# Two projection tiles per group by seven half-size products, sums of u kept on chip, and gates and a partial output parked in DRAM, in a one-core hybrid layer

## The chip, the core and the metric

One Trainium2 chip, one core. The metric is the device time of one execution in microseconds (us); less is better. TensorE (PE) multiplies matrices into PSUM, VectorE (DVE) and ScalarE (ACT) work on elements, GpSimd (POOL) and SyncE (SP) here mostly issue DMAs. Each engine runs its own queue in order; a wait at the head of a queue holds what is behind it.

## The reference

One layer over 528 tokens (16 learned ones and 512 of input), model width 1024, everything float32. Cut to what matters here:

```python
h = concat([meta, x])                       # 528 x 1024
u = rmsnorm(h, mix_norm_w)
proj = u @ w_in                             # columns: pool 1024 | z 2048 | xbc 4096 | dt 32 | gates 2048
xbc = silu(causal_depthwise_conv(xbc, conv_w, conv_b))   # xs 2048, B 1024, C 1024
dt = softplus(dt_raw + dt_bias)
y = ssd_chunked(xs, dt, -exp(a_log), B, C) + xs * d_skip # 8 groups of 4 heads, 4 chunks of 128 tokens
y = group_rmsnorm(y * silu(z)) * ssd_norm_w
y_ssd = y @ w_ssd_out
y_pool = pool_mixer(u_pool) @ w_pool_up
h = h + (sigmoid(gate_p) * y_pool + sigmoid(gate_s) * y_ssd) @ w_o
h = h + relu(rmsnorm(h) @ w_ff1)**2 @ w_ff2
out = rmsnorm(h)[16:]
```

## The kernel before

Every float32 matrix product is made of three products of rounded parts: each operand is split into a high part (a cast to fp32r on ACT, for weights at L70) and a low part (the rest, a subtraction on DVE, for weights at L71), and PE adds high·high, high·low and low·high in PSUM. u lies in SBUF already split (`uh`, `ul`, the pair `U`), 128 model columns by 528 tokens in each of 8 tiles.

**Weights** come as blocks of 128x1024 in the order in which they are used, one DMA each on SP's queue (L69). A block has a `raw` tile (3 buffers) and after the split a `whi` and a `wlo` tile (4 buffers each). One block is one 128-column tile of `w_in`, all eight 128-row steps of the contraction.

**Groups.** The scan goes by 8 groups. `group_proj(g)` (L350) makes a group's inputs: tiles B (`bt`), C (`ct`), two x tiles (`xc`, 256 columns of x in all), for some groups a gate tile (`gate_pool`, L510), and two z tiles. B, C and x each are one `proj`: 8 steps of the contraction, in each two runs of 264 (C: 258) tokens, three matmuls a run, so 48 matmuls, into one two-bank PSUM tile of `psum2`, of which there are two. Then `conv` (L327) reads that PSUM tile: an ACT activation (L329) and three DVE operations (L332), and an ACT Silu (L334) on the result. The PSUM tile is free when the third DVE operation is done.

**Order.** `weave` (L499) alternates the steps of `ssd(g)`, the scan of group g, with those of `group_proj(g + 1)`; the final order on each engine is set when the program is built, from a model of the engines' times, and is fixed on the chip. In this text weave g is the stretch in which ssd(g) runs and the inputs of group g + 1 are made. Weaves 1, 2, 3 and 5 hold a gate, weave 4 also `out_half` (L538): the output projection of groups 0 to 3, eight tiles that ACT copies from PSUM to `acc`. Weave 7 has no group left to prepare and makes `out_part` (L547), which adds groups 4 to 6 to `acc` on DVE. `ssd` gets its decay row `abc` by a DMA on POOL's queue (L389), which waits until the previous group is done with the one buffer.

**Kept in SBUF for long:** `m1` (8 gate tiles of 128x512) and `acc` (8 tiles of 128x512). The pool branch later multiplies `m1[d]` by its own product (L647).

**Start.** x^T comes in 8 tiles on SP's queue; dt's weights (128x256) on ACT's queue behind the vector of constants (L180). PE runs nine matmuls on ones and then dt and the first B tile, step by step as x^T comes.

**Behind all this** are the pool branch, the output projections, `w_o`, and the MLP, whose second product already goes by Strassen's algorithm. None of them is edited, except where `m1` and `acc` come from.

Of the kernel before, what the change touches and what calls it, by code (L numbers as in the profile page):

```python
# [42 lines left out]
WARM = 9  # L43


@with_exitstack
def kernel(ctx: ExitStack, tc, xT, x, w, vec, fnw, out):
# [25 lines left out]
    def block():  # L73
        t = block_tiles()
        block_part(t, slice(0, 1024))
        return t[2:]

# [50 lines left out]
    m1p = y_stack.enter_context(tc.tile_pool(name="m1p", bufs=1, side="right", reuse_waits="tile"))  # L128
    m1 = [m1p.tile([P, SEQ], F32, name=f"m1_{d}") for d in range(NK)]
# [50 lines left out]
    nc.scalar.dma_start(raw[:, :256], w[b, :, :256])  # L180
# [138 lines left out]
    def norm_u():  # L319
        for k in range(NK):  # L320
            dve.scalar_tensor_tensor(xt[k], xt[k], col(V_MIX, k), rsb, op0=ALU.mult, op1=ALU.mult)
            act.copy(uh[k], xt[k])
            dve.tensor_tensor(ul[k], xt[k], uh[k].bitcast(F32), op=ALU.subtract)
# [25 lines left out]
    def group_proj(g, cur, gate=None):  # L349

        first = g == 0
        xc, bt, ct, zt = cur
        for dst, t, skip in ((bt, 16 + g, 0), (ct, 24 + g, NM - 4), (xc[:, 0, :], 2 * g, 0),
                             (xc[:, 1, :], 2 * g + 1, 0)):
# [26 lines left out]
    def ssd(g, cur):  # L381
# [99 lines left out]
        qh, ql = col_sums(f"g{g}", sq[:, 0, :], gs, ("qh", "ql"))  # L481
# [28 lines left out]
    def gate_pool(d, first=False):  # L510
        ps = psum2(f"pgp{d}")[:, :SEQ]
        proj(narrow(ps), block(), X if first else U)
        if first:
            dve.tensor_tensor(m1[d], ps, rsb[:, NM:], op=ALU.mult)
        act.activation(m1[d], m1[d] if first else ps, AF.Sigmoid, bias=col(V_BG, d))
# [13 lines left out]
    accp = y_stack.enter_context(tc.tile_pool(name="accp", bufs=1, side="right", reuse_waits="tile"))  # L529
    acc = [accp.tile([P, SEQ], F32, name=f"acc{d}") for d in range(NK)]  # L530
    ys = []

# [6 lines left out]
    def out_half():  # L539
        for dd in range(4):  # L540
            ps = psum2(f"pso{dd}")
            for i in range(2):
                ssd_out(2 * dd + i, ps[:, i * SEQ : (i + 1) * SEQ], range(8))
                act.copy(acc[2 * dd + i], ps[:, i * SEQ : (i + 1) * SEQ])
                yield

    def out_part():  # L547

        un = units()
        for d in range(NK):  # L550
# [3 lines left out]
            dve.tensor_tensor(acc[d], acc[d], ps, op=ALU.add)  # L554
            yield

    for g in range(G):
        nxt = group_tiles(g + 1) if g + 1 < G else None
        fill = [group_proj(g + 1, nxt, GATE_AT.get(g))] if nxt else [out_part()]
# [81 lines left out]
    for d in range(NK):  # L641
# [5 lines left out]
        dve.tensor_tensor(m1[d], m1[d], ps, op=ALU.mult)  # L647
# [410 lines left out]
```

## Time and profile before

| what | value |
|---|---|
| median of 3 runs | 1030.96 us (1030.59 to 1031.04) |
| profiled execution, whole time | 1030.68 us |
| its span in the trace | 1029.0 us (1.7 us lie outside) |
| granted TensorE clock | 1.00 throughout |
| busy: PE, DVE, ACT, POOL | 1019.9, 711.7, 541.2, 9.9 us |
| scan stretch, weaves 0 to 6 | 67.5 to 442.0 us |

A row of a view of the trace has the start, the duration, the engine (PEld is the weight load, which runs beside PE), the line, the operation, the tiles written and read with their shapes, a count, and in brackets the idle time of the engine before it with what ended it. In the view by windows a row gives the length of a stretch and the busy time and count of each engine in it.

### The profile page before, as it was taken

What the parts mean: (1) busy time and instruction counts of PE and PEld (TensorE: products, weight loads), DVE (VectorE), ACT (ScalarE), POOL (GpSimd) and SP (SyncE); (2) the same over time, 40 slices, a digit from 0 to 9 for tenths busy, and PEclk for the clock granted to TensorE, in tenths of its full rate; (3) what the DMA queues carried; (4) which work ended last, traced back from release to release, by engine and by line L of the source; (5) the groups of instructions that cost most, each with busy time, mean ns of one, the idle gap of its engine ahead of it and who ended that gap; (6) DMA issues with size and microseconds to landing.
All of it is one profiled execution on the core that took longest, in us unless ns stands there. A gap on an engine that the chain in (4) does not pass through costs nothing.

```text
span 1029.0 us, 14033 instructions
## 1 busy us (share of the span) xinstructions
PE 1019.9 (99%) x5721; PEld 881.8 (86%) x5721; DVE 711.7 (69%) x934; ACT 541.2 (53%) x706; POOL 9.9 (1%) x24
## 2 busy tenths in 40 slices
PE   9999999999999999999999999999999999999997
PEld 8889988998879898988998888888888888888886
DVE  7978788687637586878674345646686686776866
ACT  7765967586627349573443223344545355354444
POOL 0100000000000000000000000000000000000000
PEclk9999999999999999999999999999999999999999
DMA  7332051414332321413332323543223324334112
GB/s 234 100 132 104 20 165 41 145 56 129 102 117 69 107 99 41 148 54 117 94 92 94 103 84 101 204 136 130 86 83 120 114 75 122 100 102 124 42 41 82
DMA packets 29280, 105.62 MB, mean 103 GB/s; under 512 B 3296, under 2 KB 4256, under 8 KB 28192
## 3 DMA queue, kind: packets, MB, share of 16 engines
q1 hardware_dynamic: 26352, 92.61, 28.9%
q0 software_dynamic: 2000, 11.08, 2.9%
q8 instruction: 45, 0.74, 0.3%
q10 hardware_dynamic: 864, 1.04, 0.3%
q14 instruction: 19, 0.16, 0.0%
HBM read 102.55 MB, written 2.16 MB: 102 GB/s over the span
## 4 chain that ended last, share of the span: by engine, by line
PE 98%; DVE 1%; DMA 1%; ACT 0%; SPq 0%; issue 0%; ACTq 0%; DVEq 0%
PE px L141 6%; PE px L142 6%; PE px L144 6%; PE pf L87 6%; PE pf L88 6%; PE pf L89 6%; PE alpha L801 3%; PE alpha L803 3%; PE alpha L802 3%; PE pz L141 3%; PE pz L142 3%; PE pz L144 3%; PE py L468 2%; PE pso L87 2%; PE pp L142 2%; PE pp L144 2%
## 5 line engine op out<-in xcount | busy, mean ns | idle before, releaser
L70 ACT CAST whi<-raw 128x1024 fp32r<-128x1024 f32 (+1 forms) x139 | 144.1, 1043 | 266.0 <-PE pf L88 59.9
L71 DVE TENSOR_TENSOR wlo<-raw,whi 128x1024 fp32r<-128x1024 f32 (+1 forms) x139 | 168.5, 1214 | 147.9 <-ACT whi L70 140.6
L141 PE MATMUL px<-uh,whi 128*128 128x264 f32 (+1 forms) x448 | 121.2, 290 | 0.7 <-DVE ct L332 0.7
L142 PE MATMUL px<-ul,whi 128*128 128x264 f32 (+1 forms) x448 | 118.9, 285 | 0.0
L88 PE MATMUL pf<-vl,whi 128*128 128x512 f32 x256 | 99.7, 390 | 0.0
L89 PE MATMUL pf<-vh,wlo 128*128 128x512 f32 x256 | 99.7, 390 | 0.0
L87 PE MATMUL pf<-vh,whi 128*128 128x512 f32 x256 | 99.6, 390 | 0.0
L144 PE MATMUL px<-uh,wlo 128*128 128x264 f32 (+1 forms) x448 | 90.8, 284 | 0.0
L141 PEld LDWEIGHTS px<-uh,whi 128*128 128x128 f32 x448 | 84.6, 189 | 2.8 <-issue 2.6
L142 PEld LDWEIGHTS px<-ul,whi 128*128 128x128 f32 x448 | 84.8, 189 | 0.3
L144 PEld LDWEIGHTS px<-uh,wlo 128*128 128x128 f32 x448 | 69.4, 188 | 0.3 <-issue 0.3
L752 DVE TENSOR_TENSOR slo<-b,shi 128x1024 fp32r<-128x1024 f32 x35 | 42.7, 1219 | 31.6 <-ACT shi L751 31.6
L751 ACT CAST shi<-b 128x1024 fp32r<-128x1024 f32 x35 | 36.8, 1050 | 51.9 <-PE pf L88 36.5
L88 PEld LDWEIGHTS pf<-vl,whi 128*128 128x128 f32 x256 | 48.1, 188 | 10.1 <-DVE vl L710 0.2
L89 PEld LDWEIGHTS pf<-vh,wlo 128*128 128x128 f32 x256 | 48.1, 188 | 10.0
L87 PEld LDWEIGHTS pf<-vh,whi 128*128 128x128 f32 x256 | 48.1, 188 | 9.8
L801 PE MATMUL alpha<-shi,hh 128*128 128x512 f32 x140 | 54.6, 390 | 0.0
L803 PE MATMUL alpha<-shi,hl 128*128 128x512 f32 x140 | 54.5, 389 | 0.0
L802 PE MATMUL alpha<-slo,hh 128*128 128x512 f32 x140 | 54.5, 389 | 0.0
L813 DVE TENSOR_TENSOR ht<-ht,alpha 128x1024 f32<-128x1024 f32 x35 | 42.5, 1215 | 6.1 <-PE alpha L803 6.1
L141 PE MATMUL pz<-uh,whi 128*128 128x512 f32 x112 | 44.0, 393 | 0.0
L142 PE MATMUL pz<-ul,whi 128*128 128x512 f32 x112 | 43.9, 392 | 0.0
(340 smaller groups left out, 2400.4 us busy)
## 6 DMA issues: line engine op xcount, KB each, us to landing
raw<-in_w SPq DMA_DIRECT2D x137, 512.0 KB, 3.6
b<-in_w SPq DMA_DIRECT2D x28, 512.0 KB, 3.5
abc<-acs_d POOLq DMA_DIRECT2D x8, 1024.0 KB, 7.2
xt<-in_xT SPq DMA_DIRECT2D x8, 264.0 KB, 5.4
ht<-in_x POOLq DMA_DIRECT2D x4, 512.0 KB, 5.2
w<-in_w SPq DMA_DIRECT2D x4, 512.0 KB, 3.5
out_dram<-out SPq DMA_DIRECT2D x4, 320.0 KB, 2.4
out_dram<-out ACTq DMA_DIRECT2D x4, 192.0 KB, 2.6
```

Source lines behind the costliest of these rows:

```text
L70: act.copy(hi[:, c], raw[:, c])
L71: dve.tensor_tensor(lo[:, c], raw[:, c], hi[:, c].bitcast(F32), op=ALU.subtract)
L87: pe.matmul(ps, ah, bh, start=first, stop=False)
L88: pe.matmul(ps, ah, bl, start=False, stop=False)
L89: pe.matmul(ps, al, bh, start=False, stop=last)
L141: pe.matmul(o, wh, rhs[0][k][:, c], start=k == 0, stop=False)
L142: pe.matmul(o, wh, rhs[1][k][:, c], start=False, stop=False)
L144: pe.matmul(o, wl, rhs[0][k][:, c], start=False, stop=k == NK - 1)
L752: dve.tensor_tensor(lo, src, hi.bitcast(F32), op=ALU.subtract)
L801: pe.matmul(ps[t], a[0], wh[:, cs], start=f, stop=False, skip_group_check=True)
L802: pe.matmul(ps[t], a[0], wl[:, cs], start=False, stop=False, skip_group_check=True)
L803: pe.matmul(ps[t], a[1], wh[:, cs], start=False, stop=l, skip_group_check=True)
```

## The change

1. **The two x tiles of groups 2 to 7** are no longer two `proj` but one `strassen_pair`. The 256 columns by 1024 rows of weights, and u as 1024 rows by 528 tokens, are each cut 2x2, and seven products of 128 columns by 512 rows by 264 tokens are made (Winograd's form), each 4 steps of three matmuls of 264 tokens. Four sums of weight quarters are made on DVE for each pair. The results are put together in two SBUF tiles `r1` and `r2`, partly by letting products add up in PSUM and copying the sum in between, and `conv` reads these instead of PSUM. The pair takes both `psum2` tiles.
2. **Sums of u.** Four sums of token halves and row halves of u, split high and low, are kept in 16 tiles (`T13`, `T42`). `sums_of_u` makes them once, woven into weave 0, from the unsplit u, which `norm_u` now stores to DRAM on POOL's queue and `sums_of_u` loads again on SP's queue.
3. **Room.** `m1` and `acc` leave SBUF for the length of the scan: gates and `out_half`'s tiles go through two staging tiles to DRAM on POOL's queue, and come back through them on SP's queue, in `out_part` and in the pool branch. `raw` gets a fourth buffer. GpSimd's space for DMA descriptors is halved. `qh` of the group norm shares the buffer of `xdd`.
4. **dt's weights** are the first DMA of SP's queue instead of the second of ACT's.

```diff
+RAWS = 4
+STRASSEN = range(2, G)
...
-        return (b, wp.tile([P, 1024], F32, tag="raw", name=f"raw{b}", bufs=3),
+        return (b, wp.tile([P, 1024], F32, tag="raw", name=f"raw{b}", bufs=RAWS),
...
+    def raw_block():
...
+        nc.sync.dma_start(t, w[b])
+        return t
+
+    def split_form(src, c, name):
+        hi = wp.tile([P, 1024], F32R, tag="whi", name=f"whi{name}")
+        lo = wp.tile([P, 1024], F32R, tag="wlo", name=f"wlo{name}")
+        act.copy(hi[:, c], src[:, c])
+        dve.tensor_tensor(lo[:, c], src[:, c], hi[:, c].bitcast(F32), op=ALU.subtract)
+        return hi, lo
...
-    m1p = y_stack.enter_context(tc.tile_pool(name="m1p", bufs=1, side="right", reuse_waits="tile"))
-    m1 = [m1p.tile([P, SEQ], F32, name=f"m1_{d}") for d in range(NK)]
+    stp = y_stack.enter_context(tc.tile_pool(name="stp", bufs=2, side="right", reuse_waits="tile"))
+    gate_d = [dram.tile([P, SEQ], F32, name=f"gate_d{d}") for d in range(NK)]
+    acc_d = [dram.tile([P, SEQ], F32, name=f"acc_d{d}") for d in range(NK)]
+    u_d = [dram.tile([P, L], F32, name=f"u_d{k}") for k in range(NK)]
+    def staged(name):
+        return stp.tile([P, SEQ], F32, tag="st", name=name)
...
-    nc.scalar.dma_start(raw[:, :256], w[b, :, :256])
+    nc.sync.dma_start(raw[:, :256], w[b, :, :256])
...
             dve.scalar_tensor_tensor(xt[k], xt[k], col(V_MIX, k), rsb, op0=ALU.mult, op1=ALU.mult)
+            nc.gpsimd.dma_start(u_d[k], xt[k])
...
+        pair = g in STRASSEN
+        for dst, t, skip in [(bt, 16 + g, 0), (ct, 24 + g, NM - 4)] + ([] if pair else xs):
...
+        if pair:
+            yield from strassen_pair(f"x{g}", [lambda r, d=d, t=t: conv(d, r, t) for d, t, _ in xs])
...
-        qh, ql = col_sums(f"g{g}", sq[:, 0, :], gs, ("qh", "ql"))
+        qh, ql = col_sums(f"g{g}", sq[:, 0, :], gs, ("xdd", "ql"))
...
     def gate_pool(d, first=False):
...
+        g = staged(f"gp{d}")
...
+        act.activation(g, g if first else ps, AF.Sigmoid, bias=col(V_BG, d))
+        nc.gpsimd.dma_start(gate_d[d], g)
...
+    B11, B21, B22 = quarter_of(U, 0, one), quarter_of(U, 4, one), quarter_of(U, 4, two)
+    T1, T3, T4, T2 = (quarter_of(t, 0, c) for t in (T13, T42) for c in (one, two))
+    def sums_of_u():
+        for k in range(4):
+            a, b = (rp.tile([P, L], F32, tag="r", name=f"{n}{k}") for n in ("ua", "ub"))
+            nc.sync.dma_start(a, u_d[k])
+            nc.sync.dma_start(b, u_d[4 + k])
+            dve.tensor_tensor(a[:, one], a[:, two], a[:, one], op=ALU.subtract)
+            dve.tensor_tensor(a[:, two], b[:, two], a[:, two], op=ALU.subtract)
+            dve.tensor_tensor(b[:, two], b[:, two], a[:, one], op=ALU.subtract)
+            dve.tensor_tensor(b[:, one], b[:, one], b[:, two], op=ALU.subtract)
+            for src, t in ((a, T13), (b, T42)):
+                act.copy(t[0][k], src)
+                dve.tensor_tensor(t[1][k], src, t[0][k].bitcast(F32), op=ALU.subtract)
+            yield
+    def product(ps, wf, c, b, start, stop):
+        h, l = wf
+        for k in range(4):
+            s = slice(512 * c + k * P, 512 * c + (k + 1) * P)
+            for lhs, rhs, f in ((h, b[0][k], start and k == 0), (h, b[1][k], False), (l, b[0][k], False)):
+                pe.matmul(ps, lhs[:, s], rhs, start=f, stop=stop and k == 3 and lhs is l, skip_group_check=True)
+    def strassen_pair(name, convs):
+        a1, a2 = raw_block(), raw_block()
+        sm = wp.tile([P, 1024], F32, tag="raw", name=f"rawS{name}", bufs=RAWS)
...
+        fa = split_form(a1, both, f"A{name}")
+        dve.tensor_tensor(sm[:, lo_], a2[:, lo_], a2[:, hi_], op=ALU.add)
+        dve.tensor_tensor(sm[:, hi_], sm[:, lo_], a1[:, lo_], op=ALU.subtract)
+        fs = split_form(sm, both, f"S{name}")
+        dve.tensor_tensor(a1[:, lo_], a1[:, lo_], a2[:, lo_], op=ALU.subtract)
+        dve.tensor_tensor(a1[:, hi_], a1[:, hi_], sm[:, hi_], op=ALU.subtract)
+        fd = split_form(a1, both, f"D{name}")
+        fb = split_form(a2, hi_, f"B{name}")
...
+        yz, xx = psum2(f"pyz{name}"), psum2(f"pxx{name}")
+        y, z, x = yz[:, :HALF], yz[:, 512 : 512 + HALF], xx[:, :HALF]
+        product(x, fa, 0, B11, True, False)
+        act.copy(r1[:, one], x)
+        product(y, fa, 1, B21, True, True)
+        dve.tensor_tensor(r1[:, one], r1[:, one], y, op=ALU.add)
+        product(x, fs, 1, T2, False, False)
+        act.copy(r1[:, two], x)
+        product(z, fs, 0, T1, True, False)
+        act.copy(r2[:, two], z)
+        yield
+        product(x, fd, 0, T3, False, False)
+        dve.tensor_tensor(r2[:, two], r2[:, two], x, op=ALU.add)
+        product(z, fd, 1, B22, False, True)
+        dve.tensor_tensor(r1[:, two], r1[:, two], z, op=ALU.add)
+        convs[0](r1)
+        product(x, fb, 1, T4, False, True)
+        act.copy(r2[:, one], x)
+        convs[1](r2)
+        yield
...
-                act.copy(acc[2 * dd + i], ps[:, i * SEQ : (i + 1) * SEQ])
+                a = staged(f"so{2 * dd + i}")
+                act.copy(a, ps[:, i * SEQ : (i + 1) * SEQ])
+                nc.gpsimd.dma_start(acc_d[2 * dd + i], a)
...
-            dve.tensor_tensor(acc[d], acc[d], ps, op=ALU.add)
+            a = staged(f"sa{d}")
+            nc.sync.dma_start(a, acc_d[d])
+            dve.tensor_tensor(acc[d], a, ps, op=ALU.add)
...
+        if g == 0:
+            fill.append(sums_of_u())
...
-        dve.tensor_tensor(m1[d], m1[d], ps, op=ALU.mult)
+        g = staged(f"gl{d}")
+        nc.sync.dma_start(g, gate_d[d])
+        dve.tensor_tensor(m1[d], g, ps, op=ALU.mult)
...
-    nc = bacc.Bacc("TRN2", target_bir_lowering=False, num_devices=1, dynamic_dma_scratch_size=8192)
+    nc = bacc.Bacc("TRN2", target_bir_lowering=False, num_devices=1, dynamic_dma_scratch_size=4096)
```

More of the change, by code (lines that the diff above doesn't have):

```diff
@@ L76, in block @@
         return t[2:]
+    def raw_block():
+        b = nblk[0]
+        nblk[0] += 1
+        t = wp.tile([P, 1024], F32, tag="raw", name=f"raw{b}", bufs=RAWS)
+        nc.sync.dma_start(t, w[b])
[6 more added lines that the diff above has]
+        return hi, lo
     def units():
@@ new lines @@
+    T13, T42 = ([[tf.tile([P, L], F32R, name=f"{n}{p}{k}") for k in range(4)] for p in "hl"]
+                for n in ("t13", "t42"))
+    one, two = slice(0, HALF), slice(HALF, L)
+    quarter_of = lambda t, k0, c: [[t[p][k0 + k][:, c] for k in range(4)] for p in range(2)]
+    B11, B21, B22 = quarter_of(U, 0, one), quarter_of(U, 4, one), quarter_of(U, 4, two)
[13 more added lines that the diff above has]
+            yield
```

22 lines of the change are left out of this document (15 added, 7 removed).

## The prediction

> **What bounds the kernel now.** I read the page first: span, busy shares and the chain that ended last.
>
> ```profile
> span 1029.0 us, 14033 instructions
> PE 1019.9 (99%) x5721; PEld 881.8 (86%) x5721; DVE 711.7 (69%) x934; ACT 541.2 (53%) x706; POOL 9.9 (1%) x24
> PE 98%; DVE 1%; DMA 1%; ACT 0%; SPq 0%; issue 0%; ACTq 0%; DVEq 0%
> ```
>
> PE is the bound, and by the chain 98% of the time is its own work. So a matmul less shortens the kernel by what it takes, if no other engine then comes late. DVE has 69% over the whole span, which says nothing of one stretch. So I cut the scan into its weaves (from the first transposes of ssd(g) to those of ssd(g + 1)), with one more row for the part of weave 6 from C's split to the last x matmul. Columns: length, then PE, PEld, DVE, ACT, POOL busy.
>
> ```profile
> core 0: us, PE busy (x) PEld busy (x) DVE busy (x) ACT busy (x) POOL busy (x), PEclk, DMA share, GB/s
> 67.50:111.00 43.50, 43.50 (x321) 40.16 (x320) 31.67 (x56) 29.03 (x39) 0.54 (x1) 1.00 0.27 94
> 111.00:161.50 50.50, 49.81 (x345) 45.00 (x344) 42.47 (x65) 38.98 (x56) 0.53 (x1) 1.00 0.27 84
> 161.50:211.20 49.70, 49.70 (x346) 44.98 (x345) 36.44 (x55) 33.47 (x43) 0.53 (x1) 1.00 0.31 96
> 211.20:260.30 49.10, 49.10 (x346) 44.73 (x345) 39.36 (x62) 36.91 (x49) 0.53 (x1) 1.00 0.31 97
> 260.30:348.90 88.60, 88.60 (x514) 76.49 (x513) 50.52 (x69) 43.90 (x61) 0.53 (x1) 1.00 0.33 107
> 348.90:398.50 49.60, 49.60 (x345) 44.95 (x344) 35.23 (x55) 27.54 (x39) 0.53 (x1) 1.00 0.24 75
> 398.50:442.00 43.50, 43.50 (x321) 40.19 (x320) 32.98 (x52) 29.24 (x34) 0.53 (x1) 1.00 0.36 110
> 405.30:430.60 25.30, 25.30 (x215) 24.11 (x214) 23.09 (x31) 11.25 (x15) 0.53 (x1) 1.00 0.51 157
> ```
>
> PE is busy all the time in all of them but weave 1, and there the one wait of the scan is for DVE:
>
> ```profile
> 131.07 0.36 PE L141 MATMUL px<-uh,whi 128*128 128x264 f32 x1 [0.69 <-DVE ct L332]
> ```
>
> An x tile waits for a PSUM tile that DVE's convolution of C still reads. DVE is 84% busy in that weave (42.47 of 50.50) and 91% in the stretch before the last x matmul of weave 6 (23.09 of 25.30). So DVE is the engine that is nearly late, and that is where the change adds.
>
> **PE.** The last x tile of weave 6 begins and its successor begins at
>
> ```profile
> 424.64 0.39 PE L141 MATMUL px<-uh,whi 128*128 128x264 f32 x1
> 430.61 0.40 PE L141 MATMUL pz<-uh,whi 128*128 128x512 f32 x1
> 430.84 0.40 PE L142 MATMUL pz<-ul,whi 128*128 128x512 f32 x1
> ```
>
> so 48 matmuls take 5.97 us, 0.1244 each (and one of 512 tokens 0.23). A pair goes from 2 x 48 = 96 to 7 x 4 x 3 = 84 matmuls of the same 264 tokens, each with its own weight load before and after: 12 x 0.1244 = 1.49 us less, six pairs 9.0 us. This is the whole gain. The Trainium skill ("TensorE: Matmul & The Clock Gate", Back-to-back issue gap) gives N/2.4 + 2.5 ns for an isolated matmul, 112.5 ns at N = 264; by that the gain would be an estimated 8.1 us, but the trace has 124, and the measurement decides.
>
> **DVE.** The prices, by groups of one shape and a piece of weave 6:
>
> ```profile
> L71 DVE TENSOR_TENSOR wlo<-raw,whi 128x1024 fp32r<-128x1024 f32 x137 | 167.2, 1221 | 147.7 <-ACT whi L70 140.4 <-PE po L462 7.3
> L475 DVE TENSOR_TENSOR yt<-yt,zt 128x512 f32<-128x512 f32 x16 | 10.9, 687 | 0.2
> L323 DVE TENSOR_TENSOR ul<-xt,uh 128x528 fp32r<-128x528 f32 x8 | 5.3, 699 | 0.0
> L454 DVE TENSOR_TENSOR st<-st,pst 128x256 f32<-128x256 f32 x24 | 9.9, 414 | 0.2
> 413.96 1.22 DVE L71 TENSOR_TENSOR wlo<-raw,whi 128x1024 fp32r<-128x1024 f32 x1
> 415.09 0.42 DVE L454 TENSOR_TENSOR st<-st,pst 128x256 f32<-128x256 f32 x1
> 415.69 0.75 DVE L332 SCALAR_TENSOR_TENSOR ct<-px,vs,ct 128x512 f32<-128x512 f32 x1 [0.18 <-ACT ct L329]
> 416.35 0.41 DVE L453 TENSOR_TENSOR st<-st,cdec 128x256 f32<-128x256 f32 x1
> ```
>
> A pair splits 3.5 blocks instead of 2 (1.5 x 1.22 = 1.8), makes four sums of 512 (4 x 0.69 = 2.7) and adds three PSUM results of 264, priced as 256 (3 x 0.41 = 1.2): 5.8 us. Operations overlap by about 0.08 at their ends (the split at 413.96 is followed after 1.13, not 1.22), 8.5 of them by 0.7: 5.1 us a pair. The sums of u cost 4 x (4 x 0.41 + 2 x 0.70) = 12.2, less 24 x 0.08: 10.3 us, once, in weave 0. The convolution of x reads SBUF instead of PSUM, priced the same: L454 reads PSUM and L453 does not, and they take 0.42 and 0.41.
>
> Weave by weave DVE then has, of a PE time shorter by 1.5 from weave 1 on: weave 0 42.0 of 43.5; weave 1 47.6 of 49.0; weave 2 41.5 of 48.2; 3 44.5 of 47.6; 4 55.6 of 87.1; 5 40.3 of 48.1; 6 38.1 of 42.0. In weave 0 DVE has holes which the sums can fill, since nothing needs them before weave 1's pair:
>
> ```profile
> 76.02 0.69 DVE L442 TENSOR_TENSOR cbm<-pcb,tri 128x512 f32<-128x512 f32 x1 [2.96 <-issue]
> 79.57 2.29 DVE L455 TENSOR_TENSOR abc<-abc,cbm 128x2048 f32<-128x2048 f32 x1 [2.07 <-ACT abc L434]
> 110.50 0.68 DVE L432 TENSOR_SCALAR abc<-abc,dtok 128x128 f32<-128x128 f32 x3 [3.45 <-ACT eb L424]
> ```
>
> Weaves 0 and 1 together want 89.6 us of DVE in 92.5. At the 91% of the stretch above they would take 98.5 (6 us lost), at 100% nothing is lost. I take 95%, since part of the work is free of order: 94.3, **1.8 us lost** (0 to 6). In weave 6 the stretch to the end of the pair wants 23.09 + 5.1 less the first x convolution (3 x 0.66 = 2.0 by the spacing 415.69 to 416.35), which no longer frees PSUM and can go after it: 26.2 in 23.8. Two splits for what follows (2.3) can move behind the pair too, 23.9, and at 95% that is 25.2: **1.3 lost** (0 to 2.5). The gates of weaves 1, 2, 3 and 5 and weave 4's `out_half` give DVE about 5 us of PE time or more with little to do, so there I count only the next term.
>
> **The chain inside a pair.** Product 3 adds to the PSUM bank that ACT copies after product 1, 5 waits for the copy after 3, 6 for the one after 4, 7 for a DVE addition after 5. One product of 12 x 0.124 = 1.49 us lies between each time. The copy itself is short, but ACT may be in a cast or a table load:
>
> ```profile
> L451 ACT COPY st<-pst 128x256 f32<-128x256 f32 x8 | 2.9, 366 | 2.1 <-PE pst L449 1.9
> L70 ACT CAST whi<-raw 128x1024 fp32r<-128x1024 f32 x137 | 142.9, 1049 | 265.7 <-PE pf L88 59.9 <-PE px L142 32.0 <-PE pup L88 30.7
> L334 ACT ACT_TABLE_LOAD x14 | 18.0, 1283 | 5.4 <-DVE bt L332 5.0 <-DVE xc L332 0.2
> ```
>
> Free, ACT is done 0.4 after the product; behind a whole table load 1.65, which is late by 0.2; behind a table load and a cast by 1.2. The pair also needs both PSUM tiles while C's is still read: DVE's last read of it ends 418.4 in weave 6, where the second product would begin at 416.24 + 1.49 = 417.7:
>
> ```profile
> 416.24 0.39 PE L141 MATMUL px<-uh,whi 128*128 128x264 f32 x1
> 417.67 0.75 DVE L332 SCALAR_TENSOR_TENSOR ct<-px,vs,ct 128x512 f32<-128x512 f32 x1
> ```
>
> That is late by 0.7, and here a later product on the first tile may step in. I take 0.45 a pair for all this, **2.7 us** (0 to 1.5 each, 9 in all). ACT as a whole gains 1.5 x 1.05 + 4 x 0.37 = 3.1 a pair and eight casts (5) in weave 0: at most 42 of 49 in weave 1, so it costs only in this way.
>
> **What lies aside.** 24 stores on POOL (u, gates, `out_half`) and 24 loads on SP, 256 to 264 KB each, add some 12.6 MB beside a DMA share of about 0.3; the rows
>
> ```profile
> raw<-in_w SPq DMA_DIRECT2D x137, 512.0 KB, 3.6
> abc<-acs_d POOLq DMA_DIRECT2D x8, 1024.0 KB, 7.2
> acs_d<-dacs POOLq DMA_DIRECT2D x4, 16.0 KB, 2.6
> ```
>
> put each between 2.6 and 7.2 us, nearest 3.6, against one tile in 5.5 us of PE (24 x 0.23, `out_half` and pool branch) with two staging tiles: hidden. GpSimd's halved descriptor space can make its stores follow one another, each by such a landing; the eight of u have all of weave 0. A load that waits for a staging tile holds the weights behind it on SP for at most about a tile's time, and these stand up to four buffers ahead. In `out_part` a tile is 18 x 0.23 = 4.1 us, nearer, hence 0.2 (0 to 1). dt's weights first on SP delay x^T's first tile by one issue and come earlier themselves:
>
> ```profile
> 0.81 0.39 SPq L189 DMA_DIRECT2D xt<-in_xT  x1
> 1.25 0.45 ACTq L180 DMA_DIRECT2D raw<-in_w  x1
> 4.90 0.41 ACT L197 CAST whi<-raw 128x256 fp32r<-128x256 f32 x1 [0.36 <-DMA raw<-in_w]
> ```
>
> Between -0.4 and +0.5, I take 0.
>
> **Sum.** -9.0 + 1.8 + 1.3 + 2.7 + 0.2 = -3.0. From the profiled execution, 1030.68, this gives 1027.7; the profiled execution is 0.3 below the median of the runs shown, so this counts against either. I say **1027.6 us**. What a measurement of this kernel can tell from no change is 0.2%, 2.1 us.
>
> **Rivals.**
> - *Everything is hidden.* Scheduled well, PE keeps its 100%: 1030.7 - 9.0 = 1021.7. For it: weaves 2 to 6 of before have no PE wait at all. Against: weaves 0 and 1, 97% DVE.
> - *Gain and waits cancel:* the chain terms at 1 us a pair and weaves 0 and 1 at 3: 1030.7.
> - *DVE sets the pace: slower.* In the part up to the pair's end DVE cannot be packed closer than the 91% of before, and PE stands for the rest. With the splits moved out, 23.9 / 0.913 = 26.2 against 25.3 before: +0.9 in each of weaves 2, 3, 5 and 6, 3.6; weaves 0 and 1 take 98.5 instead of 94.0, +4.5; weave 4 has room and keeps -1.0: +7.1, 1037.8. It decides as soon as a pair waits more than its 1.49 us. For it: DVE 91% there, and the 0.69 us wait. Against: much DVE work has no date.
> - *POOL's queue holds a store.* `abc` for weave 5 stands on that queue until ssd(4) frees its buffer:
>
> ```profile
> 303.51 0.53 POOL L389 DMA_DIRECT2D abc<-acs_d  x1 [65.27 <-ACT whi L70]
> ```
>
> If `out_half`'s stores are behind it, two staging and two PSUM tiles fill and PE stands, up to 303.5 - (260.3 + 4 x 5.5) = 21 us: 1043. Against: the build orders that queue by when it expects each to be ready. The Trainium skill ("SBUF — State Buffer", SBUF: two separate sides) adds that GpSimd cannot write a DMA's descriptors while DVE runs an operation that takes the port they share; in the trace abc is issued in 0.53 us in weaves full of DVE work, which does not show it.
>
> **How the numbers follow.** Forecast 0.43, all hidden 0.14, cancel 0.13, DVE 0.26, POOL 0.04. Faster: 0.57; within 0.2%: 0.13; slower: 0.30. The faster cases' own range is 1021.7 to 1028.9. The range 1022.5 to 1038.0 leaves out a twentieth below and a little over a tenth above.
>
> **What would show it.** Right: x matmuls in the scan fall from 96 to 84 a pair at 0.124; PE waits in weaves 1 to 6 sum to 5 or 6 us, in weave 1 most, behind DVE (`wlo`, sums, `ct`) and behind the copies of `pxx`; weave 2 to 5 shorter by about 1. Wrong: weaves longer than before with PE waiting for DVE; a long PE wait at `pso`; waits for `raw` or staging tiles on SP.

## The result: 1.2% slower, and the profile after

The changed kernel takes 1043.27 us (median of 4 runs, 1042.32 to 1044.22) against 1030.95 before, a ratio of 1.012 (95%: 1.0107 to 1.0133). Forecast were 1027.6 us, 1022.5 to 1038.0. Its profiled span is 1040.6 us, 11.6 more than before. The page of the changed kernel, span, busy shares and chain:

```profile
span 1040.6 us, 14179 instructions
PE 1018.0 (98%) x5649; PEld 874.9 (84%) x5649; DVE 752.1 (72%) x1012; ACT 561.9 (54%) x751; POOL 23.2 (2%) x48
PE 85%; DVE 8%; ACT 3%; DMA 2%; issue 1%; SPq 0%; ACTq 0%; DVEq 0%
```

PE has the 72 matmuls less that were forecast. Its busy time is only 1.9 us shorter, not 9.0: the two stretches of halved clock below stretch it by about 3.4, and most of the rest lies in weaves 3 to 6, where its cause is open. The chain that ended last is only 85% PE's own work, where it was 98%: DVE and ACT now stand in it. The stretches of the scan, cut at the first transposes of ssd(g) as in the prediction (weaves 4 and 5 together, since the build has moved the transposes between them), and the first part of weave 7; columns as there:

```profile
66.47:110.03 43.56, 43.56 (x321) 40.20 (x320) 38.15 (x62) 28.42 (x38) 1.09 (x2) 1.00 0.42 134
110.03:164.30 54.27, 50.13 (x334) 44.69 (x333) 51.68 (x82) 42.73 (x62) 1.10 (x2) 0.97 0.33 113
164.30:212.55 48.25, 48.25 (x333) 43.56 (x332) 42.62 (x71) 37.34 (x54) 1.09 (x2) 1.00 0.28 93
212.55:263.80 51.25, 48.84 (x334) 43.51 (x332) 41.52 (x64) 36.18 (x50) 1.09 (x2) 1.00 0.32 108
263.80:402.90 139.10, 136.41 (x833) 118.58 (x832) 97.45 (x146) 77.27 (x111) 5.97 (x11) 1.00 0.35 112
402.90:447.23 44.33, 43.06 (x310) 39.09 (x309) 37.12 (x56) 28.28 (x38) 0.55 (x1) 1.00 0.32 107
447.23:484.00 36.77, 32.72 (x174) 25.94 (x173) 29.63 (x49) 22.01 (x31) 0.00 (x0) 0.95 0.34 104
```

Against before: the start is 1.0 shorter, weave 0 the same, weave 1 3.8 longer, weave 2 1.4 shorter (the forecast saving of a pair, whole), weave 3 2.2 longer, weaves 4 and 5 0.9 longer together (two pairs should save 3.0), weave 6 0.8 longer, and everything from ssd(7) on 6.4 longer. In two stretches the granted clock is not 1.00. Against its forecast saving, weave 1 lost 5.2 us, weave 3 3.6, weaves 4 and 5 3.9, weave 6 2.3 and the part from ssd(7) on 6.4: some 21, where the forecast had 6.0. The longest PE waits of each place, from the timeline (in brackets: idle time and what ended it):

```profile
131.15 0.56 PE L592 MATMUL pxxx<-uh,whiAx 128*128 128x264 f32 x1 [2.30 <-DVE bt L357]
238.77 0.39 PE L592 MATMUL pyzx<-t13h,whiSx 128*128 128x264 f32 x1 [0.88 <-DVE r1x L613]
253.38 0.50 PE L513 MATMUL png<-qlg,ones_r 128*128 128x512 f32 x1 [1.13 <-DVE qlg L258]
341.04 0.39 PE L592 MATMUL pyzx<-uh,whiDx 128*128 128x264 f32 x1 [1.29 <-ACT r2x L617]
449.48 0.28 PE L431 MATMUL ptm<-ident,xc 128*16 128x128 f32 x1 [1.54 <-ACT xc L359]
461.92 1.04 PE L104 MATMUL psp<-yh,whi 128*128 128x512 f32 x2 [1.87 <-ACT yh L524]
```

Three kinds can be told: B's convolution late in weave 1 (131.15), products inside a pair that wait for one another's results (238.77, 341.04), and steps of the group norm and of the next ssd that come late after a pair (253.38, 449.48, 461.92).

### The profile page after: what moved, and what is told of

The parts are those of the page before. It is cut to its first block, busy times and chain, and to the rows that moved or that the text cites. A ratio compares the mean times of both kernels' runs of the same rounds, so it can differ in the third digit from the quotient of the medians.

```text
span 1040.6 us, 14179 instructions
## 1 busy us (share of the span) xinstructions
PE 1018.0 (98%) x5649; PEld 874.9 (84%) x5649; DVE 752.1 (72%) x1012; ACT 561.9 (54%) x751; POOL 23.2 (2%) x48
## 4 chain that ended last, share of the span: by engine, by line
PE 85%; DVE 8%; ACT 3%; DMA 2%; issue 1%; SPq 0%; ACTq 0%; DVEq 0%
PE pf L104 6%; PE pf L106 6%; PE pf L105 6%; PE alpha L912 3%; PE alpha L914 3%; PE alpha L913 3%; PE pxxx L592 3%; PE px L166 3%; PE px L165 2%; PE px L168 2%; PE pz L168 2%; PE pz L166 2%; PE pz L165 2%; PE pyzx L592 2%; PE pso L104 1%; PE pp L166 1%
## 5 line engine op out<-in xcount | busy, mean ns | idle before, releaser
L73 ACT CAST whi<-raw 128x1024 fp32r<-128x1024 f32 (+1 forms) x127 | 132.1, 1042 | 243.8 <-PE pf L105 59.9
L74 DVE TENSOR_TENSOR wlo<-raw,whi 128x1024 fp32r<-128x1024 f32 (+1 forms) x127 | 153.6, 1213 | 132.5 <-ACT whi L73 129.2
L165 PE MATMUL px<-uh,whi 128*128 128x264 f32 (+1 forms) x256 | 69.2, 290 | 0.0
L166 PE MATMUL px<-ul,whi 128*128 128x264 f32 (+1 forms) x256 | 67.6, 284 | 0.0
L168 PE MATMUL px<-uh,wlo 128*128 128x264 f32 (+1 forms) x256 | 51.6, 283 | 0.0
L165 PEld LDWEIGHTS px<-uh,whi 128*128 128x128 f32 x256 | 48.4, 189 | 0.4 <-issue 0.2
L166 PEld LDWEIGHTS px<-ul,whi 128*128 128x128 f32 x256 | 48.5, 189 | 0.3
L168 PE MATMUL pz<-uh,wlo 128*128 128x512 f32 x112 | 43.9, 392 | 0.0
```

The lines of the kernel that those rows point to most:

```text
L73: act.copy(hi[:, c], raw[:, c])
L74: dve.tensor_tensor(lo[:, c], raw[:, c], hi[:, c].bitcast(F32), op=ALU.subtract)
L165: pe.matmul(o, wh, rhs[0][k][:, c], start=k == 0, stop=False)
L166: pe.matmul(o, wh, rhs[1][k][:, c], start=False, stop=False)
L168: pe.matmul(o, wl, rhs[0][k][:, c], start=False, stop=k == NK - 1)
```

## The experiments

**The change taken apart.** After the result I held the three kinds of wait for the cause: the sums of u, the hand-offs inside a pair, and the weight sums' DVE time, which pushes x's convolutions back. The rival was that one of them makes nearly all of it, or that the room made for the pairs (staging through DRAM) costs something. Four kernels put the change together piece by piece; the letters are those of the expectations.

*dt_only:* the kernel before, with one line changed.

```diff
-    nc.scalar.dma_start(raw[:, :256], w[b, :, :256])
+    nc.sync.dma_start(raw[:, :256], w[b, :, :256])
```

> The kernel before with one part of the change alone: dt's weights are the first DMA of SP's queue. In the changed kernel ssd(0) began at 66.5 instead of 67.5 us. Theory A (the order of the first loads gives this 1.0 us): 1030.0. Theory B (it came from something else, the fourth raw buffer or another order of the start): 1030.9, no change.

*no_pairs:* the changed kernel without pairs, sums of u and stores of u.

```diff
-STRASSEN = range(2, G)
+STRASSEN = range(0)
-            nc.gpsimd.dma_start(u_d[k], xt[k])
-            fill.append(sums_of_u())
```

> The changed kernel without any pair, without the sums of u and without the stores of u: gates and the first half of the output still go through DRAM, four raw buffers, dt's weights first. Theory A (the loss sits in the pairs, the way through DRAM is hidden): 1029.5 to 1030.5, and PE's clock is 1.00 throughout. Theory C (the way through DRAM costs, in out_part and the pool branch above all): 1034 or more, and weave 7 to the end stays about 6 us longer than in the kernel before.

*sums_no_pairs:* only the first of these two edits, so the sums of u are made and not used.

> The changed kernel without any pair, but with the sums of u made and kept. Against the run without them this prices the sums alone. If DVE's holes in weaves 0 and 1 take them: within 0.5 us of that run, about 1030. If they crowd out DVE work with a date, as the wait of 2.3 us at the start of weave 1's pair in the changed kernel says: 2 to 4 us more, 1032 to 1034, with PE waiting in weave 1.

*no_wsums:* the changed kernel without the weight sums. Products 3 to 6 use plain quarters, so it no longer makes the x tiles; it shows time alone.

```diff
-        dve.tensor_tensor(sm[:, lo_], a2[:, lo_], a2[:, hi_], op=ALU.add)
-        dve.tensor_tensor(sm[:, hi_], sm[:, lo_], a1[:, lo_], op=ALU.subtract)
-        fs = split_form(sm, both, f"S{name}")
-        dve.tensor_tensor(a1[:, lo_], a1[:, lo_], a2[:, lo_], op=ALU.subtract)
-        dve.tensor_tensor(a1[:, hi_], a1[:, hi_], sm[:, hi_], op=ALU.subtract)
+        fs = split_form(a2, both, f"S{name}")
```

> The changed kernel with the four sums of weight quarters of each pair left out (products 3 to 6 use plain quarters): 4 x 0.6 = 2.4 us of DVE less a pair, and a shorter way to the second and third split. Theory D (DVE's amount of work in the pair stretch is the loss): 4 to 8 us less, 1035 to 1039. Theory E (the loss is in the hand-offs between products and in what the late convolutions push back on ACT): 0 to 3 us less, 1040 to 1043, with the waits for r1 and r2 still there.

| kernel | median, us | against the line above |
|---|---|---|
| before | 1030.95 | |
| + dt's weights first (dt_only) | 1029.71 | -1.2 |
| + room and staging (no_pairs) | 1030.71 | +1.0 |
| + sums of u (sums_no_pairs) | 1035.95 | +5.2 |
| + pairs, without weight sums (no_wsums) | 1033.27 | -2.7 |
| + weight sums (the change) | 1043.27 | +10.0 |

Ratios to before, for the four in that order: 0.9989 (0.998 to 0.9999), 0.9996 (0.9987 to 1.0006), 1.0047 (1.0032 to 1.0062), 1.0025 (1.0014 to 1.0036). So dt's weights first are worth 1.2 us (theory A). The +1.0 of the next line (the two kernels' times overlap) is not the way through DRAM: in the profiles no_pairs is as long as dt_only from weave 4 on, 586.9 us each from ssd(7). Its weave 0 is 2.0 longer (45.6 for 43.6, PE waits 1.6 in it), its weaves 1 to 3 are 1.3 shorter together; why weave 0 waits is open. In the lines below it weave 0 is 43.6 again, so the sums' 5.2, already more than the 2 to 4 that I expected, is too low: weave 1 grows by 7.7, from 49.3 to 57.0. The pairs without weight sums save 2.7 where 9.0 of matmul time goes. The four weight sums, 2.7 us of DVE work a pair, cost 10.0 in all (8.3 between the two profiles), which speaks against E. The profiles differ in weave 3 (51.2 to 49.1) and from ssd(7) on (593.4 to 586.9); weaves 4 to 6 keep their length (139.1 and 44.3). But 10.0 is also more than the 4 to 8 of theory D, and the edit does more than spare DVE: it frees a `raw` tile and shortens the way to the splits. What of this counts is taken up below.

**Where the sums of u cost.** In sums_no_pairs weave 1 is 57.0 us and every later weave within 0.6 us of before. DVE's order there, between the three operations of B's convolution (L357, `bt`):

```profile
127.61 0.75 DVE L357 SCALAR_TENSOR_TENSOR bt<-px,vs,bt 128x527 f32<-128x527 f32 x1
128.29 0.41 DVE L580 TENSOR_TENSOR ub<-ub,ua 128x264 f32<-128x264 f32 x1
128.63 0.75 DVE L357 SCALAR_TENSOR_TENSOR bt<-px,vs,bt 128x526 f32<-128x526 f32 x1
129.30 0.41 DVE L581 TENSOR_TENSOR ub<-ub 128x264 f32<-128x264 f32 x1
129.64 0.69 DVE L584 TENSOR_TENSOR t13l<-ua,t13h 128x528 fp32r<-128x528 f32 x1
130.26 0.74 DVE L357 SCALAR_TENSOR_TENSOR bt<-px,vs,bt 128x525 f32<-128x525 f32 x1
```

The fourth round of the sums did not fit into weave 0 and stands between operations for whose PSUM tile PE waits (2.62 us here, 2.30 in the changed kernel). Three experiments moved them.

*u_first:* `fill.insert(0, sums_of_u())` instead of `fill.append(...)`.

> The changed kernel with the sums of u put first instead of last among what is woven into weave 0, so that on DVE all four rounds stand ahead of ssd(1); in the changed kernel the fourth round stands between the three operations of B's convolution in weave 1, where PE waits 2.30 and 0.66 us and the clock is halved for 3.4 us afterwards. Theory S (what the sums cost is the place of the last round): weave 1 falls from 54.3 to about 49.5 us, weave 0 stays within 1 us of 43.6, the whole to about 1038.5 (1037.5 to 1040). Rival S' (their amount: DVE has no room for 10 us in the two weaves): weave 0 grows by what weave 1 loses, and the whole stays within 1.5 us of 1043.

1053.55 us (1049.44 to 1057.11), ratio 1.0219 (1.0189 to 1.0249): both theories missed. Now the sums stand in front of ssd(0)'s own steps, and one of them waits for its reload from DRAM at the head of DVE's queue. DVE, then PE, of u_first:

```profile
88.72 0.43 DVE L579 TENSOR_TENSOR ua<-ub,ua 128x264 f32<-128x264 f32 x1 [1.89 <-DMA ub<-u_d]
94.92 0.80 PE L512 MATMUL png<-qhg,ones_r 128*128 128x512 f32 x1 [7.91 <-ACT qhg L257]
```

PE waits 7.9 us for the group norm, and the clock is halved for three periods of 3.41 us. The reload is 1.9 of it; in the rest DVE works through sums and steps of ssd(0) by turns.

*u_pool:* the 24 operations of `sums_of_u` on `nc.gpsimd` instead of `dve`.

> The changed kernel with the sums of u (sixteen subtractions of 264, eight of 528) made by GpSimd instead of DVE, in the same place of the weave. Theory V (the sums of u cost because they stand in DVE's order between B's convolution and what waits for it): weave 1 falls from 54.3 to 49 or 50 us without a halved clock in it, the whole to about 1038 (1037 to 1040). Rival V' (GpSimd's work slows DVE's, as 128x128 operations did that took 443 instead of 272 ns beside it, or comes too late for group 2's pair): weave 1 stays above 53 us and the whole at 1042 or more.

1045.73 us (1043.27 to 1048.38), ratio 1.0144; weave 1 58.9. V fell as put, and the numbers of V' were met, though not by a slower DVE: the casts of the sums (L583) stay on ACT, in order, and wait up to 2.8 us for the slower GpSimd in front of ssd's activations.

*sums22:* sums_no_pairs, two rounds in weave 0 and two in weave 2.

```diff
-        if g == 0:
-            fill.append(sums_of_u())
+        if g in (0, 2):
+            fill.append(islice(u_rounds, 2))
```

> The sums of u without any pair, as in the run that cost 5.2 us by itself, but two rounds woven into weave 0 and two into weave 2. Theory (place): weave 1 falls from 57.0 to 49.5 us, weave 2 stays at 49 to 50, the whole is that of the run without sums and pairs, 1030.7 (1030 to 1031.5). Rival (amount of DVE work, loads and casts): 1034 to 1036.

1028.87 us (1028.32 to 1030.1): 7.1 less than sums_no_pairs with the same work. Weave 1 is 49.2 instead of 57.0, weave 2 49.1. So it is the place; the amount costs nothing that shows. It is also 1.1 below the expected range: weave 0 is 43.6, without the wait of no_pairs. This kernel, without any pair, is 2.0 faster than before.

**Hand-offs.** *y_apart:* the second product in a PSUM tile of its own.

```diff
-        y, z, x = yz[:, :HALF], yz[:, 512 : 512 + HALF], xx[:, :HALF]
+        y, z, x = psum1(f"py{name}")[:, :HALF], yz[:, 512 : 512 + HALF], xx[:, :HALF]
```

> The changed kernel with the second product's result in a PSUM tile of its own (one of the four single banks) instead of in the two-bank tile that it shares with the fourth product. Theory H (hand-offs: the fourth product of a pair waits for DVE's addition of the second, 0.88 us in weaves 3 and 6 and some 0.4 to 1.3 in 5): these waits go, 2 to 3 us faster, 1040.5 to 1041.5. Rival (the next product waits for the same late DVE, and ssd has a bank less): within 1 us of 1043.3 or slower.

1036.7 us (1035.19 to 1037.88), ratio 1.0056 (1.0041 to 1.0071): 6.6 faster than the change, more than twice what H gave. Its weaves 4 and 5, and 6:

```profile
266.57:401.51 134.94, 134.91 (x834) 118.05 (x833) 96.99 (x146) 77.15 (x110) 5.97 (x11) 1.00 0.34 116
401.51:443.83 42.32, 42.32 (x309) 38.74 (x308) 38.63 (x60) 31.15 (x42) 0.55 (x1) 1.00 0.33 116
```

139.10 became 134.94 and 44.33 became 42.32, 6.2 in all, with PE busy throughout: the three pairs there save 4.4 of the 4.5 us forecast. The 6.6 of the whole is a net figure: from ssd(7) on 3.7 go too (593.4 to 589.7), while weaves 1 and 3 are 0.8 and 2.0 longer. y and z share one tile, so the fourth product (z) waits until DVE has read y, and DVE reads it late. In weave 3 its order has weight sums in front of that addition, as the rows below show. They are not the only reason: in no_wsums, without weight sums, weaves 4 to 6 are as long as in the change. The wait at 341.04, of the sixth product for ACT's copy of z, is gone in y_apart too, with another order of products on PE: in the change the fourth (338.01) stands directly in front of the sixth, in y_apart the end of the fifth (339.75) lies between the fourth (338.29) and the sixth (340.48). DVE in weave 3 of the changed kernel, ahead of the wait at 238.77:

```profile
235.83 0.69 DVE L603 TENSOR_TENSOR raw<-raw,raw 128x512 f32<-128x512 f32 x1
236.43 0.75 DVE L501 SCALAR_TENSOR_TENSOR yt<-xc,vs,yt 128x512 f32<-128x512 f32 x1
237.09 0.68 DVE L604 TENSOR_TENSOR raw<-raw,rawSx 128x512 f32<-128x512 f32 x1
237.69 0.69 DVE L503 TENSOR_TENSOR yt<-yt,zt 128x512 f32<-128x512 f32 x1
238.29 0.42 DVE L613 TENSOR_TENSOR r1x<-r1x,pyzx 128x264 f32<-128x264 f32 x1
```

**The weight sums and what stands behind them.** *u_first_pool:* u_first with the four weight sums on `nc.gpsimd`; *apart_pool:* y_apart with the same.

> As the run with the sums of u first, and the four sums of weight quarters of each pair are made by GpSimd, which is idle for 98% of the span, instead of DVE. Theory W (the weight sums cost by the DVE time that they take from convolutions and additions, 2.7 us a pair): what leaving them out won, 10 us, is won with the sums still made, weave 7 falls from 593.4 to about 587, the whole comes to 1028 to 1031. Rival W' (the sums on GpSimd come later: each slower than DVE's 0.68 us, behind its waiting DMAs, or in DVE's way): the splits of the pair come late, PE waits for wloS and wloD, and the whole is at 1036 or more.

> All six pairs, the second product in a PSUM tile of its own, and the sums of weight quarters on GpSimd. With the tile of its own alone it was 1036.7, with 3.0 us of PE waiting for the group norm's sums in weave 3, 2.8 us in weave 7, and the dear weave 1. If the weight sums' DVE time is what makes these late, weave 3 falls from 53.3 to about 49, weave 7 to 587, the whole to 1030 to 1032. Rival: GpSimd beside DVE slows DVE, and nothing is won: 1035 to 1038.

u_first_pool: 1046.66 us (1045.09 to 1048.27), 6.9 below u_first, though far from 1028 to 1031, for which I had counted on u_first's gain; the number is the rival's, but PE does not wait for wloS or wloD. apart_pool: 1032.05 us (1031.15 to 1033.64), 4.7 below y_apart, at the upper end of the theory's range. From ssd(7) on they take 586.9 and 587.5. In apart_pool this is no gain, since weave 6 is 1.8 longer than in y_apart; the gain is weave 3, 48.4 for 53.3. *mid3* and *mid3_pool* differ in these sums' engine alone; both have y apart, the sums of u in weaves 0 and 2, and `STRASSEN = range(4, G - 1)`.

> As the run with pairs for groups 5 and 6, and group 4's pair in weave 3 too. Weave 3 was 51 to 54 us with a pair and 49.1 to 49.6 without; if its weight sums on DVE make the group norm late, it will be 51 to 53 here, and the whole 2 to 4 us above the run with two pairs (1027.5 to 1029.5); if it was late only through what earlier weaves pushed back, it will be 47.7 to 48.3 and the whole 1 to 1.5 us below (1024 to 1024.5).

> Pairs for groups 4 to 6 with the weight sums on GpSimd. By theory W (DVE's time) weave 3 is 48.3 us as in the run with six pairs and GpSimd, and the whole 1024.5; the rival (GpSimd slows DVE) gives as much as the run with the sums on DVE or more, 1027 or more.

1034.16 us (1029.46 to 1036.3) and 1025.49 us (1025.07 to 1026.61), ratios 1.003 (1.002 to 1.004) and 0.995 (0.9938 to 0.9962). mid3 is 6.6 above the run with two pairs (mid2, below), where 2 to 4 were expected; mid3_pool is 1.0 above its theory. Weaves 2 and 3 together take 105.1 and 97.0 us. What makes the group norm late can be followed back in mid3 (the first row is from the view of waits: total, times, longest):

```profile
SPq L73 <- DVE raw L605: 16.5, 1, 16.5
233.16 0.69 DVE L605 TENSOR_TENSOR raw<-raw,rawSx 128x512 f32<-128x512 f32 x1
244.93 1.05 ACT L74 CAST whi<-raw 128x1024 fp32r<-128x1024 f32 x1 [5.83 <-DMA raw<-in_w]
245.88 1.06 ACT L508 ACTIVATE sqg<-yt 128x1024 f32<-128x1024 f32 x1
246.97 0.69 DVE L509 TENSOR_TENSOR sqg<-sqg 128x512 f32<-128x512 f32 x1 [5.04 <-ACT sqg L508]
251.54 0.76 DVE L358 SCALAR_TENSOR_TENSOR xc<-r2x,vs,xc 128x526 f32<-128x526 f32 x1
252.22 0.68 DVE L259 TENSOR_TENSOR qlg<-sqg,qhg 128x512 fp32r<-128x512 f32 x1
252.96 0.79 PE L514 MATMUL png<-qlg,ones_r 128*128 128x512 f32 x1 [3.04 <-DVE qlg L259]
```

A pair holds three of the four `raw` tiles: its two blocks and the sums. SP's queue waits for DVE's last weight sum (it ends at 233.85) before it can load the next block. The loads that follow take up to 8.9 us to land, against 3.6 in the median of the whole kernel; the 1 MB of `abc` is loaded beside them, but whether that slows them was not tested. So the cast of a late block stands at the head of ACT's queue for 5.83 us. Behind the cast stands the square of the group norm (`sqg`): its input is ready at 240.46, and it starts at 245.88, with DVE idle for 5.04 us until it is done. Then come DVE's operations of x's two convolutions, which a pair makes ready together, and only then the norm's step (`qlg`) for which PE waits. In mid3_pool:

```profile
SPq L73 <- DVE wloSx L93: 14.2, 1, 14.2
239.47 1.06 ACT L508 ACTIVATE sqg<-yt 128x1024 f32<-128x1024 f32 x1
243.20 0.76 DVE L358 SCALAR_TENSOR_TENSOR xc<-r2x,vs,xc 128x526 f32<-128x526 f32 x1
243.88 0.68 DVE L259 TENSOR_TENSOR qlg<-sqg,qhg 128x512 fp32r<-128x512 f32 x1
```

DVE has the same five operations of x's convolutions in front of `qlg`, and PE does not wait once: the block alone does no harm. What is gone is the late square: SP waits for a split that ends at 230.35, ACT for no weight block longer than 0.40 us, and the square starts 0.8 us after its input is ready (238.67). The same chain stands in the changed kernel, in weaves 3 and 6:

```profile
SPq L72 <- DVE raw L604: 14.9, 1, 14.9
436.78 1.05 ACT L73 CAST whi<-raw 128x1024 fp32r<-128x1024 f32 x1 [3.88 <-DMA raw<-in_w]
437.74 1.05 ACT L507 ACTIVATE sqg<-yt 128x1024 f32<-128x1024 f32 x1
```

Six kernels with weight sums on DVE (the change, u_first, u_pool, y_apart, g2to6, mid3) have a weave with a pair in which ACT waits 2.7 to 5.8 us for a weight block directly ahead of this square; no_wsums and the five with the sums on GpSimd have no such wait over 0.5 us. The kernel before has waits of ACT for a weight block too (4.41 us in weave 1, 2.16 in weave 3), and PE's one wait in the weaves is for something else: what stands behind the cast decides. This route is read from the traces. No run tested it by itself, with a fifth `raw` tile or another place of the cast.

**The last pair.** *g2to6:* `STRASSEN = range(2, G - 1)` in the changed kernel. *late3*, *late2*, *mid2*: y apart, sums of u in weaves 0 and 2 (late2: all in weave 4), pairs for groups 5 to 7, 6 and 7, and 5 and 6.

> The changed kernel with pairs for groups 2 to 6 only; group 7's x tiles are two plain products again, in weave 6. Theory T (the late pair of group 7 pushes x's convolutions behind the start of ssd(7), and the clock is halved on top: 6.4 us in weave 7): weave 7 falls to 587, weave 6 changes by less than 1 us, the whole to about 1036.5 (1035.5 to 1038). Rival T' (weave 7 is late for the reloads of the parked tiles or for what earlier pairs pushed back): weave 7 stays above 591, and the whole is between 1042 and 1045, the 1.5 us of PE of one pair being lost.

> Pairs for groups 5 to 7 only (weaves 4, 5 and 6), the second product in a tile of its own, two rounds of the sums of u woven into weave 0 and two into weave 2. With the tile of its own, weaves 4 and 5 were 3.3 us shorter together than before the change and weave 6 1.2, weave 7 2.8 longer. Theory (the price of the sums of u is that they meet the full DVE of weave 1; where they have room they are free): 1031.0 - 1.1 for dt's weights - 3.3 - 1.2 + 2.8 = 1028.2 (1025.5 where weave 7 is not late). Rival (they cost some 5 us wherever they stand): 1033 or more.

> Pairs for groups 6 and 7 only (weaves 5 and 6), the second product in a tile of its own, all four rounds of the sums of u woven into weave 4, where DVE is busy for 57% of 88.6 us. Theory: the sums are free there; 1031.0 - 1.1 - 1.5 - 1.2 + 2.8 = 1030.0 (1027 where weave 7 is not late). Rival (sums, or their casts on ACT and loads, cost there too): 1032 or more.

> As the run with pairs for groups 5 to 7, but without group 7's pair: groups 5 and 6 only (weaves 4 and 5). Theory T (the pair in weave 6 makes what ssd(7) starts with late): weave 6 goes from 42.3 back to 43.5, weave 7 from 589.9 to 587, the whole from 1027.2 to 1025.5. Rival T' (weave 7 is late for what the change does elsewhere): weave 7 stays at 589 to 590 and the whole rises to 1028.5.

g2to6: 1038.73 us (1038.49 to 1040.98), weave 7 587.1 as T has it, the whole 2 above it, since weaves 1 and 3 were 1.6 and 2.9 longer than in the changed kernel. In weave 3 ACT waits 4.38 us for the weight block, against 2.74; for weave 1 the reason is open. late3: 1027.24 us (1026.9 to 1028.14), ratio 0.9966 (0.9953 to 0.9979), late2: 1028.72 us (1027.97 to 1030.17), 0.9981 (0.9972 to 0.999), both faster than before and a little better than their theories. mid2: 1027.55 us (1027.21 to 1028.06), between T and T': without the pair weave 6 is 1.3 longer and weave 7 1.3 shorter. So group 7's pair gives back in weave 7 what it saves, also where nothing else is late. In mid2 weave 7 still is 1.7 longer than in sums22 (PE waits 0.97 us in it, at ssd(7)'s `py`); what of the two pairs before does that is open.

**Two that put it together**, with the weight sums on GpSimd and y apart: *late4_pool*, pairs for groups 4 to 7, sums of u in weaves 0 and 2; *mid4_pool*, groups 3 to 6, sums in weaves 0 and 1.

> As the run with pairs for groups 4 to 6 and the weight sums on GpSimd, and group 7's pair in weave 6 too. Weaves 6 and 7 together were 632.5 us there, 631.7 in the run with six pairs and the weight sums on GpSimd, and 632.2 in that with pairs for groups 5 to 7 and the sums on DVE. If the pair's convolutions and weight sums make ssd(7) late as much as it saves, the whole is 1025 to 1026, the same; if the saving stands, 1024 to 1024.5.

> Pairs for groups 3 to 6, weight sums on GpSimd, two rounds of the sums of u woven into weave 0 and two into weave 1, where by DVE's order they stand behind the convolutions and not between those of B. Theory S'' (place): weave 1 stays at 49 to 50.5 us, weave 2 falls to 47.6, the whole to 1024 (1023.5 to 1025.5). Rival (amount: weave 1 has no DVE time for two rounds): weave 1 at 53 to 57 us, the whole at 1029 or more.

late4_pool 1025.48 us (1024.72 to 1025.93), the same as without group 7's pair. mid4_pool **1024.24 us** (1023.88 to 1024.77), ratio 0.9936 (0.9924 to 0.9949), faster than both given kernels. Its weave 1, and from DVE's order there two operations of the sums of u (L582, L585) and two of B's convolution:

```profile
110.42:159.65 49.23, 49.23 (x345) 44.71 (x344) 46.93 (x70) 38.96 (x54) 3.84 (x4) 1.00 0.28 92
118.00 0.36 DVE L582 TENSOR_TENSOR ub<-ub 128x264 f32<-128x264 f32 x1
123.80 0.76 DVE L358 SCALAR_TENSOR_TENSOR bt<-px,vs,bt 128x527 f32<-128x527 f32 x1
124.81 0.76 DVE L358 SCALAR_TENSOR_TENSOR bt<-px,vs,bt 128x526 f32<-128x526 f32 x1
147.11 0.70 DVE L585 TENSOR_TENSOR t13l<-ua,t13h 128x528 fp32r<-128x528 f32 x1
```

Weave 1 holds two rounds of the sums of u, DVE is 95% busy in it (46.93 of 49.23), and PE does not wait once. No operation of the sums stands inside a convolution: three subtractions of the first round come before B's, all the rest behind x's. That settles S as a matter of order. Of the 6.6 us against before, 2.0 are there without pairs (sums22); the four pairs add 4.6 of the 6.0 forecast for four, and from ssd(7) on mid4_pool is 1.7 longer than sums22.

## Why the prediction was wrong, point by point

- **PE, -9.0:** right. 72 matmuls less; where nothing else was late (weave 2; weaves 4 to 6 of y_apart together) a pair saved 1.4 to 1.5 us.
- **Sums of u, +1.8 in weaves 0 and 1:** wrong: weave 1 lost 5.2 in the change and 7.7 with the sums alone. The step that failed is "I take 95%, since part of the work is free of order". I priced a share of busy time; the queue has an order fixed by a model, and one round in the wrong place cost PE a wait of 2.3 to 2.6 us and a halved clock, while weave 1 carries two rounds at 95% without loss in mid4_pool. Weave 0 itself behaved as forecast (43.56 for 43.50).
- **DVE in weave 6, +1.3:** the wrong reason. Weave 6 was 2.3 longer than with its whole saving (44.3 for 42.0), but y_apart won 2.0 of it back with the same DVE work: it was the hand-off.
- **Chain inside a pair, 0.45 a pair, 2.7:** mis-sized. Weaves 4 to 6 alone lost 6.2, and taking the shared tile away won 6.2 back. I listed the waits of products 3, 5, 6 and 7 and left out product 4, which waits for DVE's reading of y because y and z are one PSUM tile; and I let ACT and DVE be free when asked, though both have other work in front.
- **Weight loads, 0:** wrong, and with 3.6 in weave 3 and 6.4 from ssd(7) on the largest part. I wrote of the weights that "these stand up to four buffers ahead", and looked only at staging tiles. A pair holds three of the four `raw` tiles until DVE has made its sums, SP's queue waits for the last of these (14.9 us in weave 6), the next blocks come late, and ACT's cast of one holds the group norm's square behind it. Without the sums (no_wsums) the two places fall to 49.1 and 586.9 us, with them on GpSimd (mid3_pool) weave 3 falls to 47.9. The wait for `raw` on SP was in my list of signs of being wrong. The parts overlap: y_apart also won 3.7 from ssd(7) on, so how much each is worth alone there is open.
- **x's convolutions, 0:** I counted DVE time only to the pair's end and did not ask who stands behind them. The group norm's step does; by mid3_pool this costs nothing unless the square is late already.
- **The clock:** no term. Two halved periods of 3.41 us cost about 1.7 each.
- **Staging 0.2, dt's weights 0:** nothing that shows from ssd(7) on (586.9 in no_pairs and before), and -1.2 by the medians. Weave 0 begins 1.0 earlier in the changed kernel and in dt_only, but its start varies from 66.1 to 67.3 among the kernels with dt's weights first.
- **Rivals:** "DVE sets the pace" (1037.8) named the right engine, but its mechanism, a packing limit of 91%, is refuted by 95% in mid4_pool; it also left weave 4 and the tail without loss. POOL's queue held nothing that PE felt: there is no wait at `pso`. That rival's 1043 meets the measured time by luck.

## What to carry to other kernels

Before adding work to an engine that is not the bound, look at what stands behind it in that engine's fixed order and who waits for that; a busy share says nothing of it. Count the buffers that a new block of work holds and how long: a load that waits for one of them comes late, and a step that waits for that load holds all that stands behind it in its queue. Two results in one PSUM tile with different readers are one lock. When such a change loses, move the added work (another stretch, another engine, another tile) before giving it up: here four of six pairs, with the sums of u in another place, the weight sums on another engine and y in another tile, turned 1.2% slower into 0.6% faster.

## What the runs showed of the hardware

**The clock is judged in fixed periods.** But for the last one, cut off by the end of the execution, the recorded halved periods are 3.413 us or a multiple, and lie on a grid of that length counted from the clock's first full period. Two neighbouring periods of the changed kernel (after the length comes PE busy; PEclk is third from the end):

```profile
127.72:131.14 3.42, 1.13 (x17) 0.88 (x17) 3.42 (x8) 1.39 (x3) 0.00 (x0) 0.99 0.00 0
131.14:134.55 3.41, 3.24 (x13) 2.95 (x14) 3.41 (x8) 2.41 (x3) 0.00 (x0) 0.51 0.02 5
```

Over the traces of all 20 kernels, up to 1010 us, all 14 full-clock periods with PE idle for 1.87 us or more were followed by a halved one, none of those with up to 1.57, and two of the seven between. So somewhat over half a period idle was enough. A wait costs 1.7 us more or not by where the grid cuts it: PE waits 3.04 us in weave 3 of mid3 and of y_apart; in mid3 2.92 us of idle time fall into one period and the clock is halved, in y_apart two periods have 1.66 and 1.38, and it is not. The Trainium skill ("TensorE: Matmul & The Clock Gate", "What's actually happening") has the same free-running period of 3413 ns. In "HAM oscillation — how this bites in real kernels" it asks for no idle gap over about 3.4 us; in these runs gaps of 1.9 to 3.0 us were enough to halve the clock.

**GpSimd slows some of DVE's operations and not others.** Groups of mid3, then of mid3_pool, where GpSimd makes the weight sums (1.3 to 1.6 us each, against DVE's 0.69):

```profile
L358 DVE SCALAR_TENSOR_TENSOR xc<-r2x,vs,xc 128x527 f32<-128x527 f32 x3 | 2.3, 760 | 0.0
L358 DVE SCALAR_TENSOR_TENSOR bt<-px,vs,bt 128x527 f32<-128x527 f32 x7 | 5.3, 760 | 0.5 <-ACT bt L355 0.5
L461 DVE TENSOR_SCALAR abc<-abc,dtok 128x128 f32<-128x128 f32 x64 | 13.9, 274 | 4.5 <-ACT eb L453 4.5
```

```profile
L358 DVE SCALAR_TENSOR_TENSOR xc<-r2x,vs,xc 128x527 f32<-128x527 f32 x3 | 3.3, 1109 | 0.0
L358 DVE SCALAR_TENSOR_TENSOR bt<-px,vs,bt 128x527 f32<-128x527 f32 x7 | 5.3, 761 | 0.6 <-ACT bt L355 0.6
L461 DVE TENSOR_SCALAR abc<-abc,dtok 128x128 f32<-128x128 f32 x64 | 16.9, 321 | 5.0 <-ACT eb L453 5.0
L604 POOL TENSOR_TENSOR raw<-raw,raw 128x512 f32<-128x512 f32 x3 | 4.0, 1320 | 28.1 <-DVE wloAx L93 26.6 <-issue 1.5
```

The convolution that reads SBUF twice goes from 760 to 1109 ns in the mean, the one that reads PSUM stays. A product with one tile from SBUF (L461) goes from 274 to 321. The Trainium skill ("SBUF — State Buffer", "Who interferes with whom") says that a DVE operation with two SBUF inputs contends with a GpSimd one that reads SBUF, and that one with at most one SBUF input does not, outside DVE's 2-port modes. The two convolutions agree; whether L461 runs in such a mode no trace here shows. Here the price was far below what moving the sums won.
